# Experts of a two-block transformer: four ring buffers in place of five, and TensorE's order in the expert loop by hand

## The chip, the cores and the metric

The kernel runs on one core of one Trainium2 chip. The metric is device time of that core, in microseconds; a median of runs stands for a kernel. One more execution of it was profiled, and every time below that isn't called a run's comes from that one execution. TensorE is called PE, VectorE DVE, ScalarE ACT, GpSimd POOL, and SyncE, which issues the DMAs, SP.

## What is computed

Two blocks of two layers each, batch 1, 256 tokens, model width 1024, all in float32. The first block has a mixture of experts after each of its mixers; the change lies in these two expert stages alone. Each token goes to the two best experts of the best of 4 groups of 8:

```python
def expert_block(args):
    idx, e = args
    xb = x_pad[idx]
    hdn = jax.nn.silu(xb @ w_gate[e]) * (xb @ w_up[e])
    return hdn @ w_down[e]

y = lax.map(expert_block, (buf_tok.reshape(nb, MOE_BLOCK), blk_e)).reshape(cap, d)
out = jnp.zeros((n + 1, d), x.dtype).at[buf_tok].add(y * buf_w[:, None].astype(y.dtype))
```

Gate and up are 1024 x 512, down is 512 x 1024, 2 MiB each; an expert's weights are 6 MiB, a stage's 32 experts 192 MiB. They are read from HBM once a stage.

## The kernel before

**Tiles.** An expert has 64 slots for tokens; what doesn't fit goes through a loop with a run-time count behind the 16 pairs (line 940). Experts go in pairs, so that two products of 64 rows share PE. Two pairs (four experts, 256 slots) are one q: a one-hot matrix gathers the tokens of a q with PE.

**A pair**, p of 16, runs these steps (function moe, lines 915 to 932):

- load_pair: 12 loads of 1 MiB on SP: four of gate, four of up, four of down, each half of one expert's matrix.
- gate_up: PE multiplies the gathered tokens xg with gate, then with up, into two PSUM tiles pd. Each quarter of it uses up two loads.
- slots: PE transposes the pair's one-hot weights m_PG; DVE makes from it the scatter matrix m_pgT and the gate weights m_gs.
- in odd pairs, hots and gathered: DVE builds the one-hots m_P and m_PG, PE multiplies tokens with m_P into four PSUM tiles pq, ACT writes them to a tile H, the xg of the next q.
- down, first half: ACT takes tanh of the gate, DVE makes the hidden values t2k (two operations), PE transposes them, ACT copies them to m_hT.
- down, second half: PE multiplies m_hT with the down weights into two pd; ACT and DVE split the result into a rounded part and a rest, tiles t4k.
- scatter, of the pair before: PE multiplies m_pgT with the two t4k into four pq, DVE adds each to the residual.

**Helpers.** All operations are recorded by helpers, so the profile gives few lines: 181 a DMA, 184 a product, 187 a transpose, 190 and 193 ACT, 196, 209, 213 and 216 DVE. Tiles are told apart by name.

**The ring.** A load takes the next entry of a ring of 19 buffers of 8 KB a partition (line 1840): four W, four V, S, four X, five H, and the buffer of the layer norm's rows, c_phase, which is free only when the residual has been scaled (line 917). An entry names a tag, and any free buffer of that tag serves. The tag H has 9 buffers in all (line 32) and is used for more than weights: three tiles are held through the stage (the tokens in two parts and the residual), and each xg takes one. SP issues loads in the order of the program, so a load that waits for its buffer stops those behind it. A buffer is free when PE has used what lies in it.

**The order.** The framework's scheduler puts each engine's instructions in an order of its own, from a model of their times, with the code's order as priority. It decides what is written down here only as steps.

**Buffers.** PSUM has four pd and four pq; m_pgT and m_hT have one buffer each, m_gs two, t2k three, t4k two.

Of the kernel before, what the change touches and what calls it, by code (L numbers as in the profile page):

```python
# [9 lines left out]
F32R = mybir.dt.float32r  # L10
# [7 lines left out]
P = 128  # L18
D = 1024
T = 256  # L20
# [5 lines left out]
NH_F = 2048  # L26
# [4 lines left out]
NX = 4  # L31
NH = 9
# [329 lines left out]


def mixer_a(k, x_tm, moe):

    A, nc = k.A, k.nc
# [225 lines left out]
class Moe:  # L592
# [69 lines left out]
    def run(self, r_in, bufs, then=None):  # L662

        return moe(self.k, self.l, r_in, bufs, self.gb, self.rows, self.csb, self.lps, self.lt, then)


def moe(k, l, r_in, bufs, gb, rows, csb, lps, lt, then):
# [8 lines left out]
    def ld(src, kk, n):  # L676
        w = k.wslot()[:, : kk * n].rearrange("p (k f) -> p k f", k=kk)
        k.dma(w, src)
        return w

    def load_pair(es):

        out = [([], [], []) for _ in es]
        for n, (w, kk, h) in enumerate([(wg, 8, 0), (wg, 8, 1), (wu, 8, 0), (wu, 8, 1), (wd, 4, 0), (wd, 4, 1)]):
            for j, e in enumerate(es):
                v = w[e].rearrange("(p k) f -> p k f", p=P)[:, h * kk // 2 : (h + 1) * kk // 2, :]
                out[j][n // 2].append(ld(v, kk // 2, v.shape[2]))
        return out

    ws0 = load_pair([0, 1])  # L690
# [146 lines left out]
    def gate_up(ws, xg, s0):  # L837

        gu = []
        for m in range(2):  # L840
            ps = k.pd()
            for kk in range(8):
                for j in range(2):
                    k.mm(ps[64 * j : 64 * j + 64, :], xg[:, kk, s0 + 64 * j : s0 + 64 * j + 64], ws[j][m][kk // 4][:, kk % 4, :],
                         start=kk == 0, stop=kk == 7)
            gu.append(ps)
        return gu

    def down(ws, g, u, gs):

        th = k.tl([P, 512], "t2k", NT2)
        hh = k.tl([P, 512], "t2k", NT2)
        k.act(th, g, AF.Tanh, scale=0.5)
        k.stt(hh, th, 1.0, g, ALU.add, ALU.mult)
        k.mul(hh, hh, u)
        tp = k.pq()
        for q in range(4):
            k.tr(tp[:, q * P : (q + 1) * P], hh[:, q::4])
        hT = k.tl([P, 4, P], "m_hT", 1)
        k.acopy(hT, tp.rearrange("p (q m) -> p q m", q=4))  # L860
        yp = [k.pd(), k.pd()]
        for q in range(4):
            for c in range(2):
                for j in range(2):
                    k.mm(yp[c][64 * j : 64 * j + 64, :], hT[:, q, 64 * j : 64 * j + 64],
                         ws[j][2][q // 2][:, q % 2, c * 512 : (c + 1) * 512], start=q == 0, stop=q == 3)
        yh, yl = k.tl([P, 1024], "t4k", NT4, F32R), k.tl([P, 1024], "t4k", NT4, F32R)
        for c in range(2):
            s = slice(c * 512, (c + 1) * 512)
            k.act(yh[:, s], yp[c], AF.Identity, scale=gs)  # L870
            k.stt(yl[:, s], yp[c], gs, yh[:, s], ALU.mult, ALU.subtract)
        return yh, yl

    def scatter(oh, yh, yl):

        for i in range(2):
            for c in range(2):
                s = slice(c * 512, (c + 1) * 512)
                ps = k.pq()
                k.mm(ps, oh[:, i * P : (i + 1) * P], yh[:, s], start=True, stop=False)  # L880
                k.mm(ps, oh[:, i * P : (i + 1) * P], yl[:, s], start=False, stop=True)
                k.add(r_out[:, i, s], r_out[:, i, s], ps)

    def onehots(pos_v, g_v, n):

        pt = k.tl([P, 2, n * 64], "m_P", 1, F32R)
        pg = k.tl([P, 2, n * 64], "m_PG", 1)
        v = lambda t: t.rearrange("p i (e s) -> p i e s", e=n)
        for i in range(2):
            sh = [P, n, 64]  # L890
            io = bc(iota1[:, None, :], sh)
            k.tt(v(pt)[:, i], io, bc(pos_v[:, i, :, None], sh), ALU.is_equal)
            k.mul(v(pg)[:, i], v(pt)[:, i], bc(g_v[:, i, :, None], sh))
        return pt, pg

    def transposed(pg, o):
        ps = k.pq()
        for i in range(2):
            k.tr(ps[:, i * P : (i + 1) * P], pg[:, i, o : o + P])
        return ps[:, :T]  # L900

    def slots(pg, o):

        ps = transposed(pg, o)
        oh, gs = k.tl([P, T], "m_pgT", 1, F32R), k.tl([P, 1], "m_gs", 2)
        k.red(gs, ps, ALU.add)
        k.ts(oh, ps, 0.0, ALU.is_gt)
        return oh, gs

    def hots(q):  # L910
        return onehots(pos[:, :, 4 * q : 4 * q + 4], G[:, :, 4 * q : 4 * q + 4], 4)

    def gathered(pt):
        xg = k.H()[:, :2048].rearrange("p (k s) -> p k s", k=8)
        gather(pt, 256, xg)
        return xg

    pt, pg = hots(0)
    xg = gathered(pt)
    residual(pt)  # L920
    prev = None
    for p in range(16):
        q, o = p // 2, P * (p % 2)
        ws = load_pair([2 * p, 2 * p + 1]) if p else ws0
        g, u = gate_up(ws, xg, o)
        if prev is not None:
            scatter(*prev)
        oh, gs = slots(pg, o)
        if o and q < 7:
            pt, pg = hots(q + 1)  # L930
            xg = gathered(pt)
        prev = (oh, *down(ws, g, u, gs))
    scatter(*prev)

    if then is not None:
        then()
# [3 lines left out]
    with k.tc.For_i(0, n_ov, 1) as it:  # L940
        pc = k.tl([P, 2, 1], "m_pc", 1)
        gc = k.tl([P, 2, 1], "m_gc", 1)
        V.tensor_copy(pc, pov[:, :, ds(it, 1)])
        V.tensor_copy(gc, gov[:, :, ds(it, 1)])
        e = nc.sync.value_load(evi[0:1, ds(it, 1)], min_val=0, max_val=31)
        ws = ([], [], [])
        for n, (w, kk, h) in enumerate([(wg, 8, 0), (wg, 8, 1), (wu, 8, 0), (wu, 8, 1), (wd, 4, 0), (wd, 4, 1)]):
            v = w[ds(e, 1)][0].rearrange("(p k) f -> p k f", p=P)[:, h * kk // 2 : (h + 1) * kk // 2, :]
            ws[n // 2].append(ld(v, kk // 2, v.shape[2]))
        pt, pg = onehots(pc, gc, 1)  # L950
        xg = k.H()[:, :512].rearrange("p (k s) -> p k s", k=8)
        gather(pt, 64, xg)

        half = lambda t, j: t[64 * j : 64 * j + 64]
        pg2 = k.tl([P, 2, 2, 64], "m_P", 1)
        V.tensor_copy(pg2, pg[:, :, None, :].to_broadcast([P, 2, 2, 64]))
        pgT = k.tl([P, T], "m_pgT", 1)
        k.acopy(pgT, transposed(pg2.rearrange("p i j s -> p i (j s)"), 0))
        gu = []
        for m in range(2):  # L960
            ps = k.pd()
            for kk in range(8):
                for j in range(2):
                    k.mm(half(ps, j)[:, :256], xg[:, kk, :], ws[m][kk // 4][:, kk % 4, 256 * j : 256 * j + 256],
                         start=kk == 0, stop=kk == 7)
            gu.append(ps[:, :256])
        g, u = gu
        th = k.tl([P, 512], "t2k", NT2)[:, :256]
        hh = k.tl([P, 512], "t2k", NT2)[:, :256]
        k.act(th, g, AF.Tanh, scale=0.5)  # L970
        k.stt(hh, th, 1.0, g, ALU.add, ALU.mult)
        k.mul(hh, hh, u)
        hT = k.tl([P, 4, 64], "m_hT", 1)
        for j in range(2):
            tp = k.pq()
            for q in range(4):
                k.mm(half(tp, j)[:, 64 * q : 64 * q + 64], half(hh, j)[:, q::4], half(k.ident, j)[:, 64 * j : 64 * j + 64])
            k.acopy(half(hT, j), half(tp, j)[:, :256].rearrange("p (q m) -> p q m", q=4))
        y = k.tl([P, 512], "t2k", NT2)
        yp = k.pd()  # L980
        for q in range(4):
            for j in range(2):
                k.mm(half(yp, j), hT[:, q], ws[2][q // 2][:, q % 2, 512 * j : 512 * j + 512], start=q == 0, stop=q == 3)
        k.acopy(y, yp)
        for i in range(2):
            for j in range(2):
                ps = k.pq()
                k.mm(ps, half(pgT, j)[:, i * P : (i + 1) * P], half(y, j))
                o = r_out[:, i, j * 512 : (j + 1) * 512]
                k.add(o, o, ps)  # L990
    return r_out


def mixer_c(k, x_tm, xh, xl, moe):

    A, nc = k.A, k.nc
# [833 lines left out]
def body(tc, A, out):  # L1830
    from contextlib import ExitStack

    with ExitStack() as es:
        k = K(tc, A, es)
        w = [("W", NW, k.base, 2048)] * NW
        tm = lambda: k.H()[:, :2048].rearrange("p (i d) -> p i d", i=2)
        with tc.tile_pool(name="b1", bufs=1) as b1:
            k.big = b1
            dense_ring = w + [("V", NV, b1, 2048)] * NV
            moe_ring = dense_ring + [("S", 1, b1, 2048)] + [("X", NX, b1, 2048)] * NX + [("H", NH, b1, NH_F)] * 5 + [("c_phase", 1, b1, 2048)]  # L1840
            k.set_ring(dense_ring)
            x = tm()
            k.dma(x, A["x"][0].rearrange("(i p) d -> p i d", p=P))
# [70 lines left out]
        with tc.tile_pool(name="b2", bufs=1) as b2:  # L1914
# [13 lines left out]
            for i in range(2):  # L1928
                o = b.tl([P, 1024], "Y", 6)
# [31 lines left out]
```

## Time and profile before

| what | us |
|---|---|
| runs, median of 3 (lowest to highest) | 2657.98 (2657.90 to 2659.08) |
| the profiled execution | 2663.16 |
| its span, first to last instruction | 2661.3 |
| PE busy in the span | 2487.2 (93%) |
| DVE busy | 1398.3 (53%) |
| ACT busy | 1068.1 (40%) |
| first expert stage, first product to last down product | 174.6 to 639.4 |
| second expert stage | 854.9 to 1319.8 |

The stages of the experts are 35% of the span (464.8 + 464.9 of 2661.3). Outside them the kernel has its mixers and the whole second block, which the change does not touch. A row of a timeline gives start, length, engine, line, operation, what is written and read, and in brackets how long the engine was idle before and what ended it. Rows of equal instructions that follow each other are merged: their length reaches from the first start to the last end, and rows of PE can overlap by a little. A weight product stands in the profile as two instructions, so that the 32 products of a pair's gate and up are a row of x64.

### The profile page before, as it was taken

How to read it: one execution, taken by the hardware profiler on the slowest of the kernel's cores; microseconds unless marked ns; L12 is line 12 of the kernel's file. 1: busy time of each engine (PE TensorE's matmuls, PEld its weight loads, DVE VectorE, ACT ScalarE, POOL GpSimd, SP SyncE). 2: the span in 40 equal slices, each digit the busy share in tenths (PEclk: the TensorE clock that was granted, in tenths of full speed). 3: DMA queues.
4: the chain of work that ended last, by engine and by line, in shares of the span. 5: the costliest groups of instructions: out<-in, count | busy, mean ns of one | idle time of the engine just before them, and what ended most of it. 6: DMA issues, size and time to landing. Idle time of an engine off the chain costs nothing.

```text
span 2661.3 us, 38832 instructions
## 1 busy us (share of the span) xinstructions
PE 2487.2 (93%) x15461; PEld 1786.6 (67%) x15461; DVE 1398.3 (53%) x2910; ACT 1068.1 (40%) x2134; POOL 8.0 (0%) x21
## 2 busy tenths in 40 slices
PE   8979999998777999999879999999998999999999
PEld 7744333334655333333378977899998898789999
DVE  6862222221757222221287876666557887656654
ACT  3421111111532111211158755556454875555654
POOL 0000000000000000000000000000000000000000
PEclk9989999999888999999979999999999999899999
DMA  8489799998636998999855533335553553234553
GB/s 299 154 315 422 322 397 421 421 403 345 198 112 230 421 387 340 421 421 401 340 175 173 163 112 111 112 127 163 175 171 128 184 165 111 97 126 159 175 187 115
DMA packets 189788, 645.17 MB, mean 242 GB/s; under 512 B 21618, under 2 KB 35988, under 8 KB 139556
## 3 DMA queue, kind: packets, MB, share of 16 engines
q1 hardware_dynamic: 189604, 642.66, 64.6%
q8 instruction: 123, 2.02, 0.3%
q14 instruction: 61, 0.50, 0.1%
HBM read 641.49 MB, written 1.12 MB: 241 GB/s over the span
## 4 chain that ended last, share of the span: by engine, by line
PE 47%; DVE 2%; ACT 1%; issue 0%; DMA 0%; ACTq 0%; DVEq 0%
PE pd L184 38%; PE pq L184 7%; PE pq L187 1%; ACT Y L193 1%; DVE Y L196 0%; DVE r L213 0%; ACT r L190 0%; DMA cst<-in_cst 0%; DVE H L196 0%; ACT xd L193 0%; DVE r L196 0%; DVE ln_st L295 0%; DVE lnr_t L196 0%; DVE U L196 0%; DVE cb L209 0%
## 5 line engine op out<-in xcount | busy, mean ns | idle before, releaser
L184 PE MATMUL pd<-U,Y 128*128 128x272 f32 (+1 forms) x7792 | 1030.2, 290 | 15.4 <-ACT U L193 9.2
L184 PEld LDWEIGHTS pd<-U,Y 128*128 128x128 f32 x7792 | 987.2, 190 | 46.2 <-issue 22.3
L196 DVE TENSOR_TENSOR Y<-w,Y 128x1024 fp32r<-128x1024 f32 x344 | 420.1, 1222 | 248.9 <-ACT Y L193 247.4
L184 PE MATMUL pd<-w,H 128*64 128x512 f32 (+1 forms) x2112 | 502.3, 591 | 1.1 <-DMA w<-in_moe_w_up 1.1
L193 ACT CAST Y<-w 128x1024 fp32r<-128x1024 f32 x344 | 360.1, 1047 | 339.9 <-PE pd L184 300.1
L184 PEld LDWEIGHTS pd<-w,H 128*64 128x64 f32 x2112 | 155.8, 138 | 292.4 <-issue 272.0
L184 PE MATMUL pd<-w,m_hT 128*64 128x512 f32 x1040 | 232.6, 596 | 24.4 <-ACT m_hT L193 24.4
L213 DVE SCALAR_TENSOR_TENSOR t4k<-pd,m_gs,t4k 128x512 fp32r<-128x512 f32 x64 | 48.0, 751 | 272.9 <-ACT t4k L190 270.7
L184 PEld LDWEIGHTS pd<-w,m_hT 128*64 128x64 f32 x1040 | 81.5, 137 | 152.8 <-issue 120.5
L190 ACT ACTIVATE t2k<-pd 128x512 f32<-128x512 f32 (+1 forms) x37 | 21.9, 591 | 296.0 <-PE pd L184 296.0
L190 ACT ACTIVATE t4k<-pd,m_gs 128x512 fp32r<-128x512 f32 x64 | 44.0, 687 | 210.3 <-PE pd L184 193.6
L196 DVE TENSOR_TENSOR t2k<-t2k,pd 128x512 f32<-128x512 f32 (+1 forms) x33 | 22.4, 680 | 178.4 <-PE pd L184 178.4
L196 DVE TENSOR_TENSOR H<-H,pq 128x512 f32<-128x512 f32 x132 | 83.9, 681 | 52.5 <-PE pq L184 52.2
L184 PE MATMUL pd<-Xh,H 128*128 128x512 f32 (+1 forms) x320 | 105.2, 400 | 4.0 <-ACT H L193 4.0
L193 ACT COPY m_hT<-pq 128x512 f32<-128x512 f32 (+1 forms) x34 | 19.5, 573 | 218.6 <-PE pq L187 213.7
L190 ACT ACTIVATE H<-pq,m_gb 128x256 f32<-128x256 f32 (+1 forms) x136 | 64.2, 559 | 99.5 <-PE pq L184 79.0
L213 DVE SCALAR_TENSOR_TENSOR t2k<-t2k,pd 128x512 f32<-128x512 f32 (+1 forms) x33 | 22.4, 678 | 150.5 <-ACT t2k L190 150.5
L213 DVE SCALAR_TENSOR_TENSOR r<-pd,cw,r 128x270 f32<-128x270 f32 (+1 forms) x192 | 87.9, 492 | 3.7 <-ACT r L190 2.1
L184 PEld LDWEIGHTS pq<-m_P,H 128*128 128x128 f32 x544 | 73.0, 206 | 25.1 <-issue 19.5
L184 PEld LDWEIGHTS pq<-t4k,m_pgT 128*128 128x128 f32 x256 | 43.7, 188 | 64.9 <-ACT t4k L190 20.3
L184 PE MATMUL pq<-t4k,m_pgT 128*128 128x512 f32 x256 | 80.2, 426 | 6.3 <-DVE t4k L213 6.3
L193 ACT CAST Xh<-w 128x2048 fp32r<-128x2048 f32 (+4 forms) x34 | 57.3, 1690 | 69.7 <-PE pd L184 55.1
(399 smaller groups left out, 2670.9 us busy)
## 6 DMA issues: line engine op xcount, KB each, us to landing
w<-in_moe_w_gate SPq DMA_DIRECT2D x130, 1024.0 KB, 19.9
w<-in_moe_w_down SPq DMA_DIRECT2D x130, 1024.0 KB, 19.8
w<-in_moe_w_up SPq DMA_DIRECT2D x130, 1024.0 KB, 15.7
w<-in_w_in SPq DMA_DIRECT2D x76, 1024.0 KB, 5.1
w<-in_w_mlp_up SPq DMA_DIRECT2D x32, 1024.0 KB, 5.6
w<-in_w_mlp_down SPq DMA_DIRECT2D x32, 1024.0 KB, 5.0
w<-in_w_ssd_down SPq DMA_DIRECT2D x16, 1024.0 KB, 5.8
w<-in_ev_w_in SPq DMA_DIRECT2D x14, 1024.0 KB, 13.0
```

Source lines behind the costliest of these rows:

```text
L184: return self.nc.tensor.matmul(out, l, r, start=start, stop=stop, **kw)
L187: return self.nc.tensor.transpose(out, in_, self.ident[: in_.shape[0], : in_.shape[0]])
L190: return self.nc.scalar.activation(out, in_, func, **kw)
L193: return self.nc.scalar.copy(out, in_)
L196: return self.nc.vector.tensor_tensor(out=out, in0=a, in1=b, op=op)
L213: return self.nc.vector.scalar_tensor_tensor(out=out, in0=a, scalar=s, in1=b, op0=op0, op1=op1)
```

## The change

Four things change:

- moe_ring takes four H buffers instead of five: 18 entries.
- The first half of down becomes a function of its own, hidden.
- The loop of pairs is put under a block that keeps PE to the code's order; the other engines stay with the scheduler. In the loop, the scatter of the pair before moves from behind gate_up to between hidden and down.
- m_pgT gets a second buffer, since slots now writes the next pair's before the scatter has read the last one's.

```diff
-    def down(ws, g, u, gs):
+    def hidden(g, u):
 
         th = k.tl([P, 512], "t2k", NT2)
...
         hT = k.tl([P, 4, P], "m_hT", 1)
         k.acopy(hT, tp.rearrange("p (q m) -> p q m", q=4))
+        return hT
+
+    def down(ws, hT, gs):
+
         yp = [k.pd(), k.pd()]
...
-        oh, gs = k.tl([P, T], "m_pgT", 1, F32R), k.tl([P, 1], "m_gs", 2)
+        oh, gs = k.tl([P, T], "m_pgT", 2, F32R), k.tl([P, 1], "m_gs", 2)
...
     prev = None
-    for p in range(16):
-        q, o = p // 2, P * (p % 2)
-        ws = load_pair([2 * p, 2 * p + 1]) if p else ws0
-        g, u = gate_up(ws, xg, o)
-        if prev is not None:
-            scatter(*prev)
-        oh, gs = slots(pg, o)
-        if o and q < 7:
-            pt, pg = hots(q + 1)
-            xg = gathered(pt)
-        prev = (oh, *down(ws, g, u, gs))
-    scatter(*prev)
+    with k.tc.manual_schedule(engines={mybir.EngineType.PE}):
+        for p in range(16):
+            q, o = p // 2, P * (p % 2)
+            ws = load_pair([2 * p, 2 * p + 1]) if p else ws0
+            g, u = gate_up(ws, xg, o)
+            oh, gs = slots(pg, o)
+            if o and q < 7:
+                pt, pg = hots(q + 1)
+                xg = gathered(pt)
+            hT = hidden(g, u)
+            if prev is not None:
+                scatter(*prev)
+            prev = (oh, *down(ws, hT, gs))
+        scatter(*prev)
...
-        pgT = k.tl([P, T], "m_pgT", 1)
+        pgT = k.tl([P, T], "m_pgT", 2)
...
-            moe_ring = dense_ring + [("S", 1, b1, 2048)] + [("X", NX, b1, 2048)] * NX + [("H", NH, b1, NH_F)] * 5 + [("c_phase", 1, b1, 2048)]
+            moe_ring = dense_ring + [("S", 1, b1, 2048)] + [("X", NX, b1, 2048)] * NX + [("H", NH, b1, NH_F)] * 4 + [("c_phase", 1, b1, 2048)]
```

**The gather, on PE.** This is pair 5 of the first stage, before. H_2031 is the xg that pairs 4 and 5 read, pd_2253 pair 5's gate, m_pgT_2189 the scatter matrix of pair 4, and m_P_2310 the one-hots of the next q; H_1089 and H_1090 are the tokens.

```order
L184 MATMUL pd_2253<-w_2229,H_2031 64x512
L184 MATMUL pq_2291<-t4k_2224,m_pgT_2189 128x512
L184 MATMUL pq_2295<-t4k_2224,m_pgT_2189 128x512
L184 MATMUL pq_2299<-t4k_2223,m_pgT_2189 128x512
L184 MATMUL pq_2299<-t4k_2224,m_pgT_2189 128x512
L187 MATMUL pq_2303<-ident,m_PG_2026 128x128 x2
L184 MATMUL pq_2317<-m_P_2310,H_1089 128x256
L184 MATMUL pq_2317<-m_P_2310,H_1090 128x256
```

And the same place with the change, where H_2017 is the xg of pairs 4 and 5, pd_2272 pair 5's up, and m_P_2296 the next one-hots.

```order
L184 MATMUL pd_2272<-w_2243,H_2017 64x512
L184 MATMUL pd_2272<-w_2245,H_2017 64x512
L187 MATMUL pq_2289<-ident,m_PG_2012 128x128 x2
L184 MATMUL pq_2303<-m_P_2296,H_1089 128x256
L184 MATMUL pq_2303<-m_P_2296,H_1090 128x256
```

Before, the gather begins when one product of pair 5 has been issued, and 31 more follow among and behind it; now it begins behind the last of them.

**The hidden values, on PE.** Before, at the end of the same pair: pd_2270 is its up, t2k_2362 the hidden values, m_hT_2371 their transpose.

```order
L184 MATMUL pd_2270<-w_2241,H_2031 64x512
L184 MATMUL pd_2270<-w_2243,H_2031 64x512
L187 MATMUL pq_2366<-ident,t2k_2362 128x128 x4
L184 MATMUL pd_2373<-w_2245,m_hT_2371 64x512
L184 MATMUL pd_2373<-w_2247,m_hT_2371 64x512
```

With the change, pair 5 again: t2k_2348 are the hidden values, m_hT_2357 their transpose, m_pgT_2175 and the two t4k are pair 4's.

```order
L184 MATMUL pq_2336<-m_P_2296,H_1090 128x256
L187 MATMUL pq_2352<-ident,t2k_2348 128x128 x4
L184 MATMUL pq_2359<-t4k_2225,m_pgT_2175 128x512
L184 MATMUL pq_2359<-t4k_2226,m_pgT_2175 128x512
L184 MATMUL pq_2363<-t4k_2225,m_pgT_2175 128x512
L184 MATMUL pq_2363<-t4k_2226,m_pgT_2175 128x512
L184 MATMUL pq_2367<-t4k_2225,m_pgT_2175 128x512
L184 MATMUL pq_2367<-t4k_2226,m_pgT_2175 128x512
L184 MATMUL pq_2371<-t4k_2225,m_pgT_2175 128x512
L184 MATMUL pq_2371<-t4k_2226,m_pgT_2175 128x512
L184 MATMUL pd_2375<-w_2247,m_hT_2357 64x512
```

Before, the down product stands directly behind the transposes whose copy it reads; now the eight products of the scatter stand between.

**The loads, on SP.** Before, the loads of pair 6, with the semaphores that each waits for (PE_49 is PE's, Activation_49 is ACT's, a DMAHW that of an earlier DMA). w_2401 takes the buffer in which H_2031 lay.

```order
L181 DMA w_2397<-in_moe_w_gate 128x2048 [waits DMAHW2_49,PE_49]
L181 DMA w_2399<-in_moe_w_gate 128x2048 [waits DMAHW3_49,PE_49]
L181 DMA w_2401<-in_moe_w_gate 128x2048 [waits DMAHW4_49,PE_49,Activation_49]
L181 DMA w_2403<-in_moe_w_gate 128x2048 [waits DMAHW5_49]
L181 DMA w_2405<-in_moe_w_up 128x2048 [waits DMAHW6_49]
```

With the change, the same loads:

```order
L181 DMA w_2399<-in_moe_w_gate 128x2048 [waits DMAHW2_49,PE_49]
L181 DMA w_2401<-in_moe_w_gate 128x2048 [waits DMAHW3_49,PE_49]
L181 DMA w_2403<-in_moe_w_gate 128x2048 [waits DMAHW4_49,PE_49]
L181 DMA w_2405<-in_moe_w_gate 128x2048 [waits DMAHW5_49,PE_49]
L181 DMA w_2407<-in_moe_w_up 128x2048 [waits DMAHW6_49,PE_49]
```

The load that waited for the end of pair 5's products, so that those behind it had no wait of their own left, is gone from this place; each load waits for the buffer of a weight.

## The prediction

> **What bounds the kernel now.** I began with the program's page, where one group leads.
>
> ```profile
> span 2661.3 us, 38832 instructions
> w<-in_moe_w_gate SPq DMA_DIRECT2D x130, 1024.0 KB, 19.9
> ```
>
> The span is 2661.3 us and the profiled execution took 2663.16 us, 5.18 us above the median of 2657.98 us; I subtract from the execution and carry the difference over. The second row says that an expert load moves 1 MiB and lands 19.9 us after its issue: a queue of loads stands in front of it. A pair of experts takes 12 such loads, a stage of 16 pairs takes 192.
>
> Next, busy time by stretches (columns: stretch; its length; PE, PEld, DVE, ACT, POOL busy; granted clock; DMA share; GB/s): both expert stages, and within the first a calm stretch and a hole.
>
> ```profile
> 176.40:635.20 458.80, 432.25 (x1954) 173.90 (x1951) 107.79 (x203) 66.04 (x118) 0.00 (x0) 1.00 0.97 400
> 857.60:1315.60 458.00, 431.43 (x1951) 173.68 (x1948) 107.76 (x203) 66.08 (x118) 0.00 (x0) 1.00 0.97 400
> 350.00:550.00 200.00, 187.41 (x838) 75.38 (x838) 43.97 (x79) 28.10 (x50) 0.00 (x0) 1.00 1.01 421
> 325.00:350.00 25.00, 23.40 (x105) 8.62 (x102) 3.83 (x7) 6.21 (x12) 0.00 (x0) 1.00 0.56 226
> ```
>
> PE is busy 94% of both stages, which looks like the bound, but DMA runs at 400 of its 421 GB/s. A load at 421 GB/s takes 1,048,576 B / 421 = **2.49 us**, so a pair needs 12 x 2.49 = 29.9 us of DMA, and two pairs 59.8. PE's pace before is seen in its timeline (start, length, engine, line, out<-in, [idle before]):
>
> ```profile
> 395.05 0.72 PE L187 MATMUL pq<-ident,t2k 128*128 128x128 f32 x4 [0.87 <-DVE t2k L196]
> 396.51 7.14 PE L184 MATMUL pd<-w,m_hT 128*64 128x512 f32 x32 [0.73 <-ACT m_hT L193]
> 405.29 1.07 PE L184 MATMUL pd<-w,H 128*64 128x512 f32 x2
> 455.20 0.72 PE L187 MATMUL pq<-ident,t2k 128*128 128x128 f32 x4 [0.87 <-DVE t2k L196]
> ```
>
> From one hidden transpose to the one two pairs later PE takes 455.20 - 395.05 = 60.15 us. So PE and DMA go at almost the same pace, and a faster PE alone would only wait for weights. What can be won is DMA time that is lost now. The sync engine's issues show where it goes:
>
> ```profile
> 155.93 22.66 SPq L181 DMA_DIRECT2D w<-in_moe_w_up  x4
> 175.47 3.12 SPq L181 DMA_DIRECT2D w<-in_moe_w_up  x2
> 856.64 2.25 SPq L181 DMA_DIRECT2D w<-in_moe_w_up  x2
> 250.70 24.20 SPq L181 DMA_DIRECT2D w<-in_moe_w_up  x4
> 302.94 32.91 SPq L181 DMA_DIRECT2D w<-in_moe_w_gate  x4
> 555.23 20.79 SPq L181 DMA_DIRECT2D w<-in_moe_w_gate  x4
> ```
>
> Four neighbouring loads that take 24.2, 32.9 and 20.8 us to issue hold a stop, longer than the queue's 19.9 us. The middle one empties it: 226 GB/s in the row of 325 to 350 above. The order shown with the change names the stop: a load (w_2401) waits for the tokens H_2031 to be dead, because the next tokens H_2316 were gathered while H_2031 was still read and took a buffer of the ring.
>
> **Term 1, the stops go.** Lost time by the rates: 458.8 x (1 - 400/421) = **22.9 us** in the first stage, 458.0 x (1 - 400/421) = **22.8 us** in the second. After the change the gather stands behind all gate and up products of an odd pair, so the old tokens are dead when the new are written; 4 ring buffers, 3 held tiles and 2 of tokens fill the 9 exactly. Nothing then holds back the loads, if the ring of 18 keeps the queue fed. In two pairs PE frees 24 buffers in less than DMA's 59.8 us (term 2), so the backlog only grows; the tight place is the first odd pair, whose gate and up products are this row:
>
> ```profile
> 197.71 13.90 PE L184 MATMUL pd<-w,H 128*64 128x512 f32 x64
> 213.50 0.38 PE L187 MATMUL pq<-ident,m_PG 128*128 128x128 f32 x2
> ```
>
> They end at 211.6; the next buffers come half a down product later, after slot transposes (0.38), gather (4.04), hidden transposes (0.7), scatter (2.11) and half of 7.09, all rows of term 2: 10.8 us, at 222.4. By then 21 loads are free to go since 176.4, work until 176.4 + 21 x 2.49 = 228.7. The cover is 6 us; without it each us of lack costs one.
>
> **Term 2, PE's pace.** The start of each stage runs unbroken already, and shows what the written order gives:
>
> ```profile
> 869.65 0.75 PE L187 MATMUL pq<-ident,t2k 128*128 128x128 f32 x4 [0.45 <-DVE t2k L196]
> 878.00 13.90 PE L184 MATMUL pd<-w,H 128*64 128x512 f32 x64
> 893.94 4.04 PE L184 MATMUL pq<-m_P,H 128*128 128x256 f32 x32
> 899.57 7.09 PE L184 MATMUL pd<-w,m_hT 128*64 128x512 f32 x32 [1.10 <-ACT m_hT L193]
> 906.49 13.90 PE L184 MATMUL pd<-w,H 128*64 128x512 f32 x64
> 920.32 2.11 PE L184 MATMUL pq<-t4k,m_pgT 128*128 128x512 f32 x8
> 923.91 7.09 PE L184 MATMUL pd<-w,m_hT 128*64 128x512 f32 x32 [0.73 <-ACT m_hT L193]
> 930.83 1.02 PE L184 MATMUL pd<-w,H 128*64 128x512 f32 x2
> ```
>
> Two unbroken pairs take 930.83 - 878.00 = 52.83 us. (Broken ones are dearer: two weight products alone, at 405.29, last 1.07, while 64 last 13.90, 0.43 for two.) The scatter of 2.11 now covers both waits for m_hT, 1.10 and 0.73; in the even pair the hidden transposes keep the 0.45 wait of the row at 869.65. That is 52.83 - 1.83 + 0.45 = **51.5 us**, 25.7 a pair. From the first product at 174.6, 16 pairs would end at 586. But the last weights can't land before about 615 (term 3): PE catches up with the loads after half of the stage and waits then, so its gain of 60.15 - 51.5 = 8.6 us in two pairs is not added to the sum. The covers are ACT's: behind the gather it evacuates in 3.75 us what PE gathers in 4.04, then copies m_hT under the scatter. DVE's four additions of the scatter, 2.48, fall under the down product of 7.09, ahead of its evacuation.
>
> ```profile
> 328.33 3.75 ACT L190 ACTIVATE H<-pq,m_gb 128x256 f32<-128x256 f32 x8
> 349.06 2.48 DVE L196 TENSOR_TENSOR H<-H,pq 128x512 f32<-128x512 f32 x4 [3.44 <-PE pq L184]
> ```
>
> Should ACT lag, a pair has 29.9 - 25.7 = 4.2 us to spare before it shows.
>
> **Term 3, one load later.** The 155.93 and 175.47 rows say that of pair 1's four up loads the last two came at 175.47 and after: 12 + 4 + 2 = 18 were issued by then, and the next took the buffer of the rows of the layer norm (the ring's last entry), free only at 175.47, and at 856.64 in the second stage. With 4 H buffers that entry comes one load earlier: 175 instead of 174 loads remain, **+2.49 us** a stage. The last landing moves from 635.2 to 635.2 - 22.9 + 2.5 = 614.8, and from 1315.6 to 1295.3.
>
> **Term 4, the end of a stage.** Both stages end on DMA already:
>
> ```profile
> 625.82 3.65 PE L184 MATMUL pd<-w,H 128*64 128x512 f32 x14 [0.53 <-DMA w<-in_moe_w_up]
> 631.72 7.68 PE L184 MATMUL pd<-w,m_hT 128*64 128x512 f32 x32 [0.73 <-ACT m_hT L193]
> 1306.15 3.65 PE L184 MATMUL pd<-w,H 128*64 128x512 f32 x14 [0.53 <-DMA w<-in_moe_w_up]
> 1312.07 7.69 PE L184 MATMUL pd<-w,m_hT 128*64 128x512 f32 x32 [0.73 <-ACT m_hT L193]
> 635.45 0.52 POOL L1017 MEMSET phase<- 33x512 f32 x1 [634.49 <-DMA w<-in_moe_w_down]
> ```
>
> PE resumes when the last up weights land and ends 13.58 us later (639.40 - 625.82). Now the previous pair's scatter, 2.1, stands before the last down product in place of the 0.73 wait, and the 0.6 by which that product stretched (7.68 against 7.09) goes: **+0.7 us** a stage. A wait put on PE here delays only the product behind it, and the final scatter.
>
> The second slot buffer (m_pgT) costs nothing: PE finds it written long before. The order also lets one half-size projection load pass two small ones after the first stage: at most 0.5 MiB / 421 = 1.2 us, below a chain on DVE of 13.49 us:
>
> ```profile
> 682.69 3.54 PE L187 MATMUL pq<-ident,H 128*128 128x128 f32 x15 [13.49 <-DVE H L196]
> ```
>
> I take 0, and keep -1 to +1.2 in the range.
>
> **Sum.** Stage 1: 22.9 - 2.5 - 0.7 = 19.7; stage 2: 22.8 - 2.5 - 0.7 = 19.6. 2663.16 - 39.3 = 2623.9, or **2619 us** beside the median.
>
> **A clock that falls, the rival that ends slower.** Once PE waits for weights, it works 13.90/4 = 3.5 us and waits 2 x 2.49 - 3.5 = 1.5, over and over. These stretches show what such a pattern may do:
>
> ```profile
> 334.40:337.80 3.40, 1.80 (x9) 0.90 (x10) 0.69 (x1) 0.59 (x1) 0.00 (x0) 1.00 0.52 142
> 337.80:341.20 3.40, 3.40 (x18) 1.15 (x16) 0.00 (x0) 0.00 (x0) 0.00 (x0) 1.00 1.02 424
> 641.00:645.00 4.00, 2.15 (x15) 1.62 (x13) 3.13 (x10) 0.00 (x0) 0.00 (x0) 1.00 0.38 133
> 645.00:648.00 3.00, 3.00 (x16) 3.00 (x16) 0.00 (x0) 0.00 (x0) 0.00 (x0) 0.51 0.95 303
> ```
>
> After 3.4 us with 53% busy the clock stays at 1.00; after 4.0 us with 54% it is 0.51. With waits of 1.5 a stretch of 3.4 us can be 56% busy: near the edge. A stretch of 3.4 us at half clock loses 1.7 us of work. A pair has 4.2 to spare, and some 7 pairs a stage wait, so it decides from 3 such stretches of a pair's 9; at 4.4 the gain is gone; at six the cost is (6 x 1.7 - 4.2) x 14 = 84, **2703 us**. Against it: a cold PE falls behind, its waits vanish, and it is fully busy, as in the last row; so it heals itself. The Trainium skill (TensorE: Matmul & The Clock Gate, "HAM oscillation — how this bites in real kernels") asks for no PE gap above about 3.4 us; by that rule waits of 1.5 cost nothing and the sum stands, while the 645.00 row, behind a largest gap below 2 us, is harsher. No more hangs on the page.
>
> **Other rivals.** *The stops stay*: tokens still take a ring buffer. Then terms 3 and 4 alone remain: 2658 + 2 x 3.2 = **2664**. The order on record speaks against it. *Half of the stops return* in the shorter ring: 2619 + 22.8 = **2642**; against it the 6 us of cover and its growth. *A new PE wait* of over 4.2 us a pair, say 5.5 (a PSUM buffer that ACT frees late): 1.3 x 32 = 42 back, **2660**, no change; the cover above speaks against it.
>
> **Chances.** Forecast 0.81; half of the stops 0.09; PE wait 0.04; stops stay 0.03; clock 0.03. A measurement of this kernel tells some 0.2% (5 us) from no change: faster 0.90, same 0.04, slower 0.06. The range: at the low end every lost microsecond by the count of loads, 458.8 - 174 x 2.49 = 25.5 a stage, returns: 2658 - 2 x 25.5 + 6.4 = 2613, less 2; at the high end a third of the stops returns with some cold stretches, 2619 + 17 = 2636.
>
> **What would show it.** The changed profile should hold 421 GB/s from about 177 to 613 us without a hole; issues in steps of 2.49 with no stop above 10 us; the first stage's last down product ending near 620 instead of 639; PE's idle time moved from m_hT and t2k to w, some 1.5 us at a time, from about pair 9. Wrong would be: a hole in GB/s (the ring), PEclk below 0.95 in the stages (the clock), or a PE wait on pq that grows.

## The result and the profile after

| | before | changed |
|---|---|---|
| runs, median of 4 (lowest to highest), us | 2658.47 (2657.90 to 2659.08) | 2620.20 (2617.68 to 2631.31) |
| ratio, 95% interval | | 0.9859 (0.9843 to 0.9875) |
| the profiled execution, us | 2663.16 | 2617.68 |
| first stage, first gate product to end of the last down product, us | 464.8 | 445.7 |
| second stage, us | 464.9 | 447.1 |

The change takes 38.3 us from the median, 1.4%; 39.3 were forecast. The stages give 19.1 and 17.8 us of it. The two profiled executions differ by 45.5 us: the other 8.5 lie outside the stages, and most of them turn up below as the spread of single executions.

The windows of the changed kernel (stretch; its length; PE, PEld, DVE, ACT, POOL busy; granted clock; DMA share; GB/s), a piece of the first stage, both stages, and what follows them:

```profile
325.00:350.00 25.00, 24.55 (x116) 9.21 (x114) 6.11 (x11) 3.25 (x5) 0.00 (x0) 1.00 1.01 421
172.40:618.06 445.66, 415.84 (x1978) 169.01 (x1977) 109.89 (x210) 67.32 (x122) 0.82 (x2) 1.00 1.00 416
832.05:1279.15 447.10, 416.68 (x1978) 169.73 (x1977) 110.61 (x214) 67.33 (x122) 0.00 (x0) 1.00 1.00 414
1279.15:2615.90 1336.75, 1292.38 (x9691) 1169.83 (x9691) 911.00 (x1853) 780.06 (x1628) 3.73 (x11) 0.98 0.45 146
```

The same view of the kernel before:

```profile
174.59:639.40 464.81, 438.26 (x1978) 176.55 (x1977) 109.65 (x210) 67.75 (x121) 0.82 (x2) 1.00 0.96 396
854.88:1319.76 464.88, 438.31 (x1978) 176.64 (x1977) 110.53 (x214) 67.90 (x122) 0.00 (x0) 1.00 0.96 396
1319.76:2661.30 1341.54, 1297.25 (x9691) 1175.71 (x9691) 911.44 (x1853) 779.61 (x1628) 3.73 (x11) 0.98 0.45 145
```

The hole of 226 GB/s is gone, and the sync engine's issues hold no stop of 20 us (start, length of four issues in a row; the stage's longest gap between two, 9.6 us, lies within this row):

```profile
209.45 11.39 SPq L181 DMA_DIRECT2D w<-in_moe_w_gate  x4
```

But PE's busy time fell as well, by 22.4 us in the first stage (438.26 - 415.84) for the same 1978 recorded instructions. Which of the two counted is seen in the waits of PE within the first stage: first the kernel before (what waited, for whom; us in total, times, longest), then the changed one.

```profile
PE pd L184 <- ACT m_hT L193: 12.0, 16, 1.1
PE pq L187 <- DVE t2k L196: 11.2, 14, 0.9
PE pq L184 <- DVE t4k L213: 2.9, 10, 0.3
PE pd L184 <- DMA w<-in_moe_w_up: 0.5, 1, 0.5
```

```profile
PE pd L184 <- DMA w<-in_moe_w_up: 18.6, 15, 1.3
PE pd L184 <- DMA w<-in_moe_w_gate: 6.6, 4, 2.7
PE pq L187 <- DVE t2k L196: 3.9, 9, 0.5
PE pd L184 <- ACT m_hT L193: 0.7, 1, 0.7
```

Before, PE waited for a weight once in the stage, for 0.5 us, in the last pair. The stops in the loads held up loads, not PE. Now PE waits for weights 25 us a stage (25.2 and 25.7). So the bound moved from PE's order to the loads, and the question for the experiments is whether the ring had any part in it.

PE's timeline with the change, as it still has weights (the hidden transposes of two even pairs, and the gate and up products of the odd pair between them) and later:

```profile
288.83 0.75 PE L187 MATMUL pq<-ident,t2k 128*128 128x128 f32 x4 [0.45 <-DVE t2k L196]
298.28 13.90 PE L184 MATMUL pd<-w,H 128*64 128x512 f32 x64
...
340.34 0.75 PE L187 MATMUL pq<-ident,t2k 128*128 128x128 f32 x4 [0.45 <-DVE t2k L196]
...
407.61 4.70 PE L184 MATMUL pd<-w,H 128*64 128x512 f32 x18
415.01 3.65 PE L184 MATMUL pd<-w,H 128*64 128x512 f32 x16 [2.70 <-DMA w<-in_moe_w_gate]
420.00 3.65 PE L184 MATMUL pd<-w,H 128*64 128x512 f32 x16 [1.33 <-DMA w<-in_moe_w_up]
424.96 3.65 PE L184 MATMUL pd<-w,H 128*64 128x512 f32 x14 [1.31 <-DMA w<-in_moe_w_up]
...
604.01 3.65 PE L184 MATMUL pd<-w,H 128*64 128x512 f32 x14 [1.31 <-DMA w<-in_moe_w_up]
610.97 7.09 PE L184 MATMUL pd<-w,m_hT 128*64 128x512 f32 x32
```

Two pairs take 340.34 - 288.83 = 51.51 us, and 51.5 was forecast. From pair 7 (counted from 0) PE meets the loads: a quarter of the products runs 3.65 us and waits 1.3, together about two loads' 4.98 us.

### The profile page after: what moved, and what is told of

The parts are those of the page before. It is cut to its first block, busy times and chain, and to the rows that moved or that the text cites. A ratio compares the mean times of both kernels' runs of the same rounds, so it can differ in the third digit from the quotient of the medians.

```text
span 2615.9 us, 38872 instructions
## 1 busy us (share of the span) xinstructions
PE 2435.3 (93%) x15461; PEld 1763.0 (67%) x15461; DVE 1398.0 (53%) x2910; ACT 1067.4 (41%) x2134; POOL 8.1 (0%) x21
## 4 chain that ended last, share of the span: by engine, by line
PE 46%; DVE 2%; ACT 1%; DMA 1%; issue 0%; ACTq 0%; DVEq 0%
PE pd L184 38%; PE pq L184 7%; PE pq L187 1%; ACT Y L193 1%; DVE Y L196 0%; DVE r L213 0%; ACT r L190 0%; DMA cst<-in_cst 0%; DVE r L196 0%; DMA csd<-cr 0%; DMA cr<-csd 0%; DVE H L196 0%; DVE U L213 0%; ACT sg L190 0%; DVE Z L196 0%
## 5 line engine op out<-in xcount | busy, mean ns | idle before, releaser
L184 PE MATMUL pd<-w,H 128*64 128x512 f32 (+1 forms) x2112 | 481.5, 591 | 51.2 <-DMA w<-in_moe_w_up 37.0
L184 PEld LDWEIGHTS pd<-w,m_hT 128*64 128x64 f32 x1040 | 71.7, 137 | 142.7 <-issue 138.8
L196 DVE TENSOR_TENSOR t2k<-t2k,pd 128x512 f32<-128x512 f32 (+1 forms) x33 | 22.4, 680 | 226.4 <-PE pd L184 226.4
L213 DVE SCALAR_TENSOR_TENSOR t2k<-t2k,pd 128x512 f32<-128x512 f32 (+1 forms) x33 | 22.4, 680 | 217.1 <-ACT t2k L190 217.1
L196 DVE TENSOR_TENSOR H<-H,pq 128x512 f32<-128x512 f32 x132 | 82.0, 682 | 26.5 <-PE pq L184 26.5
L193 ACT COPY m_hT<-pq 128x512 f32<-128x512 f32 (+1 forms) x34 | 19.5, 573 | 173.3 <-PE pq L187 168.3
L184 PE MATMUL pd<-Z,Y 128*128 128x272 f32 (+1 forms) x512 | 84.4, 286 | 0.0
L196 DVE TENSOR_TENSOR Xl<-w,Xh 128x2048 fp32r<-128x2048 f32 (+4 forms) x34 | 68.7, 2023 | 23.5 <-ACT Xh L193 23.3
L184 PE MATMUL pq<-m_P,H 128*128 128x256 f32 (+1 forms) x544 | 72.7, 295 | 3.7 <-DVE m_pos L196 2.0
```

What stands on the lines that cost most here:

```text
L184: return self.nc.tensor.matmul(out, l, r, start=start, stop=stop, **kw)
L193: return self.nc.scalar.copy(out, in_)
L196: return self.nc.vector.tensor_tensor(out=out, in0=a, in1=b, op=op)
L213: return self.nc.vector.scalar_tensor_tensor(out=out, in0=a, scalar=s, in1=b, op0=op0, op1=op1)
```

## The experiments

Two theories. **A**, the prediction's: the stages were long because load time was lost at the stops, so what takes the stops away wins. **B**, from the waits above: they were long because PE's order needed 60.15 us for two pairs, so what brings PE below the loads' 59.8 us wins, whatever the ring does.

Each ratio is to runs of the kernel before that were made beside the run in question; the runs were made in three sets, in which the kernel before has medians of 2658.47, 2661.01 and 2660.51 us.

| run | median, us | ratio to before, 95% | stage 1 / stage 2, us | two pairs on PE, weights there, us | PE's waits for weights, stage 1, us |
|---|---|---|---|---|---|
| before | 2658.47 | | 464.8 / 464.9 | 60.2 | 0.5 |
| changed | 2620.20 | 0.9843 to 0.9875 | 445.7 / 447.1 | 51.5 | 25.2 |
| changed, again | 2618.85 | 0.9835 to 0.9860 | 445.6 / 446.9 | 51.5 | 25.1 |
| order, five H | 2619.99 | 0.9834 to 0.9861 | 445.3 / 444.2 | 51.4 | 22.6 |
| ring of four alone | 2652.16 | 0.9957 to 0.9981 | 463.2 / 463.0 | 59.2 to 60.2 | 0 |
| scatter at its old place | 2622.10 | 0.9838 to 0.9868 | 445.9 / 446.1 | 52.8 | 18.2 |
| ring without H | 2643.18 | 0.9918 to 0.9945 | 455.7 / 457.5 | 51.5 | 31.8 |
| new code, scheduler's order | 2623.10 | 0.9841 to 0.9869 | 445.6 / 447.7 | 55.9 to 58.2 | 3.0 |
| five H in the first round | 2618.13 | 0.9825 to 0.9851 | 443.1 / 444.8 | 51.4 | 20.6 |

### The order alone, the ring alone

The first takes the changed kernel and gives the ring its fifth H buffer back, the second takes the kernel before and only shortens the ring.

```diff
-            moe_ring = dense_ring + [("S", 1, b1, 2048)] + [("X", NX, b1, 2048)] * NX + [("H", NH, b1, NH_F)] * 4 + [("c_phase", 1, b1, 2048)]
+            moe_ring = dense_ring + [("S", 1, b1, 2048)] + [("X", NX, b1, 2048)] * NX + [("H", NH, b1, NH_F)] * 5 + [("c_phase", 1, b1, 2048)]
```

> The changed kernel with five H buffers in the ring again: TensorE's written order alone. Theory A (what ended the stages before was load time lost at the stops): a gather that comes behind all gate and up products finds the old tokens dead, but its new tile still takes a ring buffer, so stops may remain; if they stay as long as before (20 us and more), 2650 to 2660 us. Theory B (what ended them was PE's own pace of 60.15 us for two pairs; PE waited only 0.52 us for weights in the whole stage): the order is the whole gain, 2613 to 2622 us, at most a short hole of 2 to 3 us in the loads, paid for by one load more that is issued ahead (2.49 us a stage).

```diff
-            moe_ring = dense_ring + [("S", 1, b1, 2048)] + [("X", NX, b1, 2048)] * NX + [("H", NH, b1, NH_F)] * 5 + [("c_phase", 1, b1, 2048)]
+            moe_ring = dense_ring + [("S", 1, b1, 2048)] + [("X", NX, b1, 2048)] * NX + [("H", NH, b1, NH_F)] * 4 + [("c_phase", 1, b1, 2048)]
```

> The kernel before with four H buffers in the ring, nothing else: the scheduler's order of PE stays. Theory A (stops): no issue gap above 10 us, DMA at 421 GB/s without a hole, and the whole gain, 2619 to 2625 us. Theory B (PE's pace): the holes go or shrink but PE still needs some 60 us for two pairs and waits for no weights; each stage lasts 460 to 466 us and the time is 2650 to 2663 us.

The order alone gave everything, 2619.99 us, with gaps of 9.2, 13.7 and 11.2 us back between issues of the first stage; before they were 19.4, 29.6 and 19.5. The shorter gaps left no hole in the load rate, which was 421 GB/s from 200 to 600 us. This is the stretch that had 226 GB/s before, first with the order alone, then with the ring alone:

```profile
325.00:350.00 25.00, 24.56 (x116) 9.20 (x114) 6.03 (x10) 2.56 (x4) 0.00 (x0) 1.00 1.01 421
```

```profile
325.00:350.00 25.00, 23.40 (x106) 8.81 (x104) 6.12 (x10) 6.20 (x12) 0.00 (x0) 1.00 1.01 420
```

So the order by itself made PE faster and ended the holes too, and its run alone does not tell the two theories apart. The ring alone does: it ended the holes and left PE's order. It gave 0.3%, and 1.6 and 1.9 us in the stages; the rest of its gain lies outside them, where single executions differ by as much (below). PE's waits in the first stage, ring alone:

```profile
PE pd L184 <- ACT m_hT L193: 12.2, 16, 1.1
PE pq L187 <- DVE t2k L196: 11.2, 14, 0.9
PE pq L184 <- DVE t4k L213: 2.8, 10, 0.3
```

Two rows of its PE in that stage, two pairs apart:

```profile
335.05 0.72 PE L187 MATMUL pq<-ident,t2k 128*128 128x128 f32 x4 [0.87 <-DVE t2k L196]
394.20 0.72 PE L187 MATMUL pq<-ident,t2k 128*128 128x128 f32 x4 [0.87 <-DVE t2k L196]
```

And the issue of the stage's last four loads, in the kernel before and with the ring alone:

```profile
608.45 7.79 SPq L181 DMA_DIRECT2D w<-in_moe_w_down  x4
```

```profile
592.61 4.60 SPq L181 DMA_DIRECT2D w<-in_moe_w_down  x4
```

No gap between its issues is longer than 10.9 us, and its last load is issued 19.0 us sooner than before (597.21 against 616.24 at the rows' ends): of the 22.9 - 2.5 = 20.4 us that the prediction counted, the loads did get 19.0 back. PE went on at 59.2 to 60.2 us for two pairs, waited for no weight at all, and its stage was 1.6 us shorter. The weights came sooner and lay ready for longer. Theory A falls, theory B stands. What stops as long as those before would do to the faster PE, no run shows.

### The scatter's place

The changed kernel with the scatter behind gate_up again, where the old code had it, but in the written order:

```diff
             g, u = gate_up(ws, xg, o)
+            if prev is not None:
+                scatter(*prev)
             oh, gs = slots(pg, o)
...
             hT = hidden(g, u)
-            if prev is not None:
-                scatter(*prev)
             prev = (oh, *down(ws, hT, gs))
```

> The changed kernel with the scatter of the pair before put back behind the gate and up products, still in the written order, so that the waits for m_hT are uncovered again. If the loads bound the stages now: 2617 to 2622 us, no change against the changed kernel; two pairs of PE cost 53.3 instead of 51.5 us while it has weights, and it waits that much less for weights. If PE's pace still counted: 1.8 us x 8 x 2 stages = 29 us more, 2649 us.

PE's waits in its first stage:

```profile
PE pd L184 <- ACT m_hT L193: 14.4, 16, 1.1
PE pd L184 <- DMA w<-in_moe_w_up: 11.6, 11, 1.3
PE pd L184 <- DMA w<-in_moe_w_gate: 6.6, 4, 2.7
PE pq L187 <- DVE t2k L196: 0.4, 1, 0.4
```

The waits for m_hT are back, 14.4 us in place of 0.7; those for t2k, which the scatter now covers, fell from 3.9 to 0.4, and those for weights from 25.2 to 18.2. The stages moved by 1 us at most. What the moved scatter covers is time that PE would otherwise wait for loads.

### PE without the loads' bound

To see PE's pace by itself, four kernels leave out the down weights' loads; the gate tiles are multiplied in their place, so a pair loads 8 MiB. There is one run of each, and their stage is the first.

```diff
-                out[j][n // 2].append(ld(v, kk // 2, v.shape[2]))
+                if n < 4:
+                    out[j][n // 2].append(ld(v, kk // 2, v.shape[2]))
+        for o in out:
+            o[2].extend(t.rearrange("p k f -> p (k f)").rearrange("p (k f) -> p k f", k=2) for t in o[0])
```

> The changed kernel with the down weights' loads left out (the gate tiles are used in their place), so that a pair loads 8 MiB instead of 12 and PE never waits for weights: this shows PE's pace by itself. Expected 51.5 us for two pairs from first to last (the prediction's term 2), a stage of 16 x 25.75 + 6 = 418 us, against 445.7 and 447.1 in the changed kernel. If PE's pace were set by the loads in some other way than by waits for weights (the same memory is written while PE reads), two pairs would take less than 51.3.

It took 2541.94 us: 51.35 us for two pairs nearly throughout, 406.9 us for the stage. (The forecast of 418 added 6 us for the stage's ends, which cost nothing extra; and the first and last steps of two pairs take 50.28 and 48.18 us only.) So the changed kernel's PE could do a stage in 407 us and is held to 446 by the loads: of the 57.9 us that the order saves PE (464.8 - 406.9), 38.8 are given back as waits for weights, 25.2 of them shown as idle time. The rest is in PE's busy time, 415.8 us against 406.9 - 4.6 of idle = 402.3 here: products that last longer where waits break them up. In pair 9, the rows from 407.61 on, the four stretches between waits are busy 4.70 + 3 x 3.65 = 15.65 us with the 32 products that take 13.90 unbroken.

The other three put a piece of the scheduler's old order back by hand, still without down loads. The gather (ga) and the scatter (st) become generators that stop after each product, some(it, n) makes the next n of them, and gate_up does so ahead of the product that a table names:

```diff
+                    for f in cuts.get(16 * m + 2 * kk + j, ()):
+                        f()
```

The tables of the three, in this order odd cuts, even cuts, and the scatter:

```python
cuts = {1: [lambda: some(ga, 10)], 8: [lambda: some(ga, 4)], 9: [lambda: some(ga, 99)]}
cuts = {2: [lambda: some(ga, 10)], 8: [lambda: some(ga, 4)], 10: [lambda: some(ga, 99)]}
cuts = {0: [lambda: some(st, 4)], 1: [lambda: some(st, 9)]}
```

> The same without down loads; in odd pairs the gather is laid among the gate products at the places that the scheduler chose before: ten products of it behind the first gate product, four behind the eighth, eighteen behind the ninth. Theory B1 (PE runs two products of 64 rows side by side, and a cut behind an odd number leaves one alone): cuts behind 1, 8 and 9 cost 0.6 to 0.7 us for each product left alone, some 2 to 3 us in two pairs: 53.5 to 54.5 us. Theory B2 (broken products were slow before only because weights came late): 51.5 us, no change, since weights are there.

> As the run before, with the cuts behind an even number of products: behind 2, 8 and 10. Theory B1: no product is alone, 51.5 to 52 us for two pairs. Rival: every change between gather and gate costs whatever its place, the same 2 to 3 us as with odd cuts.

> The same without down loads; the gather stands behind the products, but the scatter of the pair before lies where the scheduler had it: four products ahead of the first gate product, four behind it. Theory B1: each pair pays 0.6 us for the two products left alone, 0.3 us for t4k, and 0.73 us for m_hT, which is uncovered again, about 2 x 1.7 = 3.4 us less the 0.45 covered: 54.5 to 55.5 us for two pairs. With the gather's 2 to 3 us that would make up most of the 60.15 - 51.5 = 8.65 us; what is left is the wait of 0.87 us for t2k that ends every pair before.

| left out: down loads | run, us | stage, us | two pairs, us |
|---|---|---|---|
| order by hand | 2541.94 | 406.9 | 51.35 |
| gather, even cuts | 2573.68 | 423.0 | 53.65 |
| gather, odd cuts | 2602.03 | 434.9 | 55.35 |
| scatter, odd cut | 2649.62 | 459.1 | 58.33 |

Rows of an odd pair with odd cuts, then with even cuts, then of a pair with the scatter cut:

```profile
364.57 1.07 PE L184 MATMUL pd<-w,H 128*64 128x512 f32 x2
366.94 3.65 PE L184 MATMUL pd<-w,H 128*64 128x512 f32 x14
371.19 1.07 PE L184 MATMUL pd<-w,H 128*64 128x512 f32 x2
374.51 10.51 PE L184 MATMUL pd<-w,H 128*64 128x512 f32 x46
385.89 0.73 PE L187 MATMUL pq<-ident,t2k 128*128 128x128 f32 x4 [0.87 <-DVE t2k L196]
```

```profile
358.27 1.08 PE L184 MATMUL pd<-w,H 128*64 128x512 f32 x4
360.64 2.79 PE L184 MATMUL pd<-w,H 128*64 128x512 f32 x12
364.03 1.08 PE L184 MATMUL pd<-w,H 128*64 128x512 f32 x4
367.33 9.66 PE L184 MATMUL pd<-w,H 128*64 128x512 f32 x44
377.90 0.72 PE L187 MATMUL pq<-ident,t2k 128*128 128x128 f32 x4 [0.91 <-DVE t2k L196]
```

```profile
345.83 1.34 PE L184 MATMUL pq<-t4k,m_pgT 128*128 128x512 f32 x3 [0.28 <-DVE t4k L213]
347.11 1.07 PE L184 MATMUL pd<-w,H 128*64 128x512 f32 x2
349.24 13.95 PE L184 MATMUL pd<-w,H 128*64 128x512 f32 x62
365.44 7.09 PE L184 MATMUL pd<-w,m_hT 128*64 128x512 f32 x32 [0.73 <-ACT m_hT L193]
```

One product by itself (x2) takes 1.07 us and two (x4) take 1.08: two products of 64 rows run side by side, and one alone costs as much as two. The Trainium skill (TensorE: Matmul & The Clock Gate, "Part 3: Packing small matmuls — row/col tiling") states that products on different parts of the array run at the same time, and these rows agree. The 32 products take 16.30 us with odd cuts, 14.61 with even ones, 13.90 uncut. The two kernels with the gather differ by 55.35 - 53.65 = 1.70 us, and their weight products by 16.30 - 14.61 = 1.69: that is the price of the odd places.

All three forecasts were too low. Even cuts (51.5 to 52 forecast) cost 2.3 us: 0.7 in the weight products, 0.5 in the gather's own three pieces (4.53 us against 3.99 in one), and 0.9 because the gather no longer stands between the products and the hidden transposes, so that t2k is waited for (0.91). Odd cuts (53.5 to 54.5 forecast) pay the last two as well. The scatter's cut (54.5 to 55.5 forecast) had its waits for t4k and m_hT in the forecast, but not the scatter's own pieces, 6.03 us for two pairs against 4.19, and its weight products cost 1.07 + 13.95 - 13.90 = 1.1 us a pair instead of 0.6. That weights came late is no part of the old order's price, since here they were there.

### How long the ring must be

```diff
-            moe_ring = dense_ring + [("S", 1, b1, 2048)] + [("X", NX, b1, 2048)] * NX + [("H", NH, b1, NH_F)] * 4 + [("c_phase", 1, b1, 2048)]
+            moe_ring = dense_ring + [("S", 1, b1, 2048)] + [("X", NX, b1, 2048)] * NX + [("H", NH, b1, NH_F)] * 0 + [("c_phase", 1, b1, 2048)]
```

> The changed kernel with no H buffer in the ring (14 entries instead of 18): a large step of term 3. Theory A and B both have the stages bound by loads now: four loads fewer are issued ahead of each stage, 4 x 2.49 x 2 = 19.9 us more, 2640 us. By the prediction's cover of 6 us at the first odd pair, which shrinks by four loads of 2.49 us, a hole of some 4 us a stage comes on top: 2648 us. Rival: the ring's length does not matter as long as the queue is fed, 2620 us.

The stages of this kernel:

```profile
175.09:630.75 455.66, 419.35 (x1978) 170.50 (x1977) 109.74 (x210) 67.24 (x121) 0.82 (x2) 1.00 1.00 416
845.14:1302.66 457.52, 420.74 (x1978) 169.74 (x1977) 110.52 (x214) 67.16 (x122) 0.00 (x0) 1.00 1.00 413
```

They are 10.0 and 10.4 us longer for four loads fewer, 2.5 to 2.6 us a load, as term 3 has it, and at 416 and 413 GB/s for the stages (416 and 414 in the changed kernel) there is no extra hole (422 GB/s from 200 to 250 us, around the first odd pair): the cover there was larger than the 6 us that the prediction counted. The median is 23 us above the changed kernel's, of which the stages explain 20.4.

### The block, and a longer first round

The loop of the change without the block; the code in it stays as it is.

```diff
-    with k.tc.manual_schedule(engines={mybir.EngineType.PE}):
-        for p in range(16):
+    for p in range(16):
```

> The changed kernel without the block that keeps PE to the code's order: the code still has the scatter behind the hidden values and the ring has four H buffers, but the scheduler places PE's work. It lays the gather into the down product ahead of an odd pair and behind its first gate product, and leaves one product alone in two pairs or so. If only PE's pace against 59.8 us for two pairs matters: some 52 to 57 us, below 59.8, so the loads bound the stages and it takes 2618 to 2625 us, no change against the changed kernel. Rival: the written order is what counts, and the pace is back at 60: 2650 us.

It took 2623.10 us. PE needs 55.9 to 58.2 us for two pairs, below 59.8, so the stages stay at 445.6 and 447.7 us; but its waits for weights are 3.0 us only, so it has almost nothing to spare. With the ring of four, moving the code was enough; the block gives the room.

Then the fifth H buffer in the ring's first round alone, and beside it the changed kernel once more:

```diff
-            moe_ring = dense_ring + [("S", 1, b1, 2048)] + [("X", NX, b1, 2048)] * NX + [("H", NH, b1, NH_F)] * 4 + [("c_phase", 1, b1, 2048)]
+            ring = lambda n: dense_ring + [("S", 1, b1, 2048)] + [("X", NX, b1, 2048)] * NX + [("H", NH, b1, NH_F)] * n + [("c_phase", 1, b1, 2048)]
+            moe_ring = ring(5) + ring(4) * 10
```

> The changed kernel, with five H buffers in the ring's first round only (19 entries, then rounds of 18). The loads bound the stages, and no tokens have taken a second H buffer during the first round: one load more is issued ahead, 174 instead of 175 remain, and no stop follows. 2 x 2.49 = 5.0 us less than the changed kernel on the same chip, some 2615 us, 443 to 444.5 us a stage. Rival: the stops of the five-buffer ring return (9 to 14 us between issues, as with five buffers throughout) and nothing is won.

> The changed kernel once more, beside the other two on the same chip: 2618 to 2623 us, stages of 445 to 447.5 us; what lies outside the stages shows how much of the 8.5 us that the profiled execution of before lost there belongs to that one execution.

With five in the first round the stages are 2.5 and 2.1 us shorter than those of the changed kernel beside it, one load of 2.49 each, as expected. The median does not show it: 2618.13 (2614.56 to 2619.13) against 2618.85 (2617.95 to 2624.09). What follows the second stage varies by as much from execution to execution: the same 9691 matmuls there last 1342.18 us in the profiled execution of this kernel, 1337.03 in that of the changed kernel beside it, 1336.75 in the changed kernel's first and 1341.54 before. So 4.8 of the 8.5 us that the executions of before and after differ by outside the stages is such a spread, whose cause was not looked for. Of the rest, 2.2 lie ahead of the first stage, which begins at 172.40 and 174.43 us in the two executions of the changed kernel and at 174.59 before: a spread as well. No version beats the changed kernel by what can be measured.

## Why the prediction came out right, and what was wrong in it

**The total**: 2619 forecast, 2620.2 measured, in a range of 2611 to 2636. By stage: 19.7 and 19.6 us forecast, 19.1 and 17.8 measured; the 1.8 us that the second stage lacks aren't explained.

**The signs came, and could not tell.** The prediction asked for 421 GB/s without a hole, no stop above 10 us, a first stage that ends near 620 us and PE's idle time moved to the weights. All of it came (421, 9.6, 618.06, 25.2 us). But a PE that was the bound before, and is so no longer, gives the same signs. It took the ring alone to tell the two causes apart.

**Term 1 named the wrong cause.** The step that failed is "What can be won is DMA time that is lost now", with "a faster PE alone would only wait for weights" ahead of it and "Term 1, the stops go" behind it. The lost DMA time was counted about right, 20.4 us net, and 19.0 of it came back when only the ring was shortened; but the stage was only 1.6 us shorter for it. And the new order, with the ring left at five, gave the whole gain. The right step starts from the only wait for a weight in the stage before, 0.5 us, which the prediction quoted as the stage's end and did not read further: the stage was PE's, 438.3 us busy and 26.5 idle, all but 0.5 of it behind ACT and DVE. The gain is then 464.8 less the larger of two times: PE's new need, 406.9, and that of loads without holes, 464.8 - 19.7 = 445.1 by the prediction's terms and 445.7 measured.

That the number agrees is in part luck. The end that the prediction worked out, the last load's landing and what follows it, is the one that held afterwards. But it got there by taking what the loads had lost off a time that PE had set, and this comes out only because the two were level before: the last load landed 4 us ahead of PE's end (635.2 against 639.4). Why they were level was not tested; the loads were held by tokens that PE gave free at its own pace, which would do it.

**Readings of rows.** The stops themselves were 19.4, 29.6 and 19.5 us; of the three only the middle one is longer than the 19.9. What the prediction calls two weight products alone, the row at 405.29, is one product in two instructions, so a product alone costs 1.07 us where one in an unbroken run costs 0.43. In the clock's sum the whole gain of 39.3 us is gone at 4.1 cold stretches a pair, not at 4.4.

**Term 2, PE's pace**: 51.5 forecast, 51.4 to 51.5 measured. That the gain ends at the loads' bound was right. But without the faster PE next to nothing was won (1.6 and 1.9 us), where the prediction counted none of it in the sum. PE met the loads at pair 7 instead of 9 and waited 1.3 us a time instead of 1.5. The old order's surplus, 60.15 - 51.35 = 8.8 us in two pairs, is by the rows 3.5 in the weight products (31.32 us against 2 x 13.90), 3.3 in waits (m_hT 1.5, t2k 1.2 more than now, t4k 0.6) and 1.6 in the pieces of scatter and gather; 0.4 are not placed. The pieces put back by hand, 4.0 us for the gather and 7.0 for the scatter, are together more than 8.8, so their prices can't be added; why was not looked for.

**Term 3, one load later**: right, 2.49 us a load; 2.5 to 2.6 with four, 2.1 and 2.5 with one.

**Term 4, the stage's end**: 0.7 us forecast; the last quarter of the products to the end of the down product took 13.58 us before and 618.06 - 604.01 = 14.05 after, 0.5.

**The second m_pgT and the moved projection load** at nothing: what lies between the stages took 215.5 us before, and 214.0 and 214.1 in the two profiled executions of the changed kernel; no cost shows.

**The rivals.** Stops that stay or half return were not seen at their full length: with five buffers gaps of up to 13.7 us returned, the load rate kept to 421 GB/s, and the stages were no longer than with four. A hole that cost load time would count now, since the loads set the end, as four loads fewer ahead did: 10 us a stage. A new wait on pq did not show. The clock stayed at 1.00 in both stages with waits of 1.3 us, so the cold stretches that the prediction priced from a stretch with 54% busy did not come (below). A rival that was missing is the one that held: the loads were not the bound before.

## What to carry to other kernels

A hole in the load rate is a loss only where the consumer waits for that load: read the consumer's waits by releaser before counting GB/s, since loads that stop because their buffers are full cost nothing while PE has its weights: the ring alone brought the loads 19.0 us and the stage 1.6. When two resources need 60.15 and 59.8 us, take each one's own need apart (run it with less of the other) and forecast the larger of the two afterwards, not the sum of what each loses. And where half-height products run side by side, lay other work between them only behind an even number, and rather not at all: three even cuts still cost 0.7 us in the products here.

## What the runs showed of the hardware

In these rows the clock does not follow the busy share of the stretch just before. In the changed kernel's first stage, and behind it in the loop for what doesn't fit an expert's slots:

```profile
411.40:414.80 3.40, 0.91 (x6) 0.03 (x2) 0.00 (x0) 0.00 (x0) 0.00 (x0) 1.00 1.01 414
414.80:418.20 3.40, 3.19 (x16) 1.19 (x16) 0.00 (x0) 0.00 (x0) 0.00 (x0) 1.00 1.01 419
622.00:624.00 2.00, 1.22 (x11) 1.22 (x11) 0.89 (x7) 0.00 (x0) 0.00 (x0) 1.00 0.97 291
624.00:626.00 2.00, 2.00 (x18) 2.00 (x18) 0.00 (x0) 0.00 (x0) 0.00 (x0) 0.89 0.79 262
626.00:628.00 2.00, 1.61 (x9) 1.45 (x8) 0.29 (x1) 0.66 (x3) 0.00 (x0) 0.50 0.99 414
```

With 27% busy and a gap of 2.70 us the clock stayed at 1.00, in that stretch and the next; around 625 us it fell to 0.50 behind a gap of 1.72 us, the largest there, though PE was busy 61% of 2 us and then all of the next 2. By the rule of the Trainium skill that the prediction weighed (TensorE: Matmul & The Clock Gate, "HAM oscillation — how this bites in real kernels": no gap above some 3.4 us) the first is as it should be; the second is not explained by it, nor by any run here.
